# Paired 64-row score products, one reciprocal for two rows and a reordered seam in a decoder-layer kernel

## The chip, the cores and the metric

The kernel runs on one core of a Trainium2 chip. The metric is the device time of one execution in microseconds (us); the median of the runs counts. A difference is given with an interval where several rounds were run.

## What is computed

One decoder layer on 1024 tokens of width 1024, everything in float32. An input projection feeds two mixers. The first is sparse attention: 8 heads in 2 groups of 4, head size 64, with a compressed branch (63 keys), a selected branch and a window branch (512 keys back), each head and branch with its own gate. With 16 blocks of 64 keys and 16 blocks selected, the selected branch sees every causal key. The second is latent attention with 8 heads of 96 score dimensions. Then an output projection, a layer norm, a gated feed-forward part of width 2816, a layer norm, and a gated embedding with a third norm. The part that the change touches, cut down:

```python
s = jnp.einsum('bqghd,bkgd->bqghk', qblk, kwb).astype(f32)
bias = -slopes[:, :, None] * dist[:, None, None, :].astype(f32)
p = _masked_softmax(s + bias, mask)
o_win = jnp.einsum('bqghk,bkgd->bqghd', p.astype(vwb.dtype), vwb)
...
o = g[..., 0:1] * o_cmp + g[..., 1:2] * o_slc + g[..., 2:3] * o_win
...
gu = x @ w_up[i]
ffn = (jax.nn.silu(gu[..., :D_FF]) * gu[..., D_FF:]) @ w_down[i]
```

## The kernel before, in words

Products in float32 are made from two parts of each operand, a high part (rounded to fp32r) and a low part (the rest). ScalarE writes the high part (`hi`, L103), VectorE subtracts to get the low part (`lo`, L109), and `mm3` (L120) multiplies high by high, high by low and low by high (L122, L123, L124).

**Sparse heads.** A query tile holds 128 rows for a head of 64: one half has the high part of q, the other half the low part; which half is which goes by the parity of the head (`evac_q`, L308). The key tiles hold the high part twice (`KS[g][0]`, `KW[g][0]`) and the low part twice (`KS[g][1]`, `KW[g][1]`), on both halves (`evac_k`, L320). So the scores of one head take two products of 128 rows: q by the high keys gives high times high plus low times high; q by the low keys gives high times low plus low times low.

**Units and groups.** A unit is one head, one block of 128 queries (`qb`) and one branch (the compressed and the selected branch share one: 64 compressed columns, the "head", stand ahead of `n = 128*(qb+1)` selected ones; the window has up to 640). Four units, the heads of one group, make a Group; there are 32 sparse groups, ordered `qb` 0 to 7 for the first and 7 to 0 for the second head group, and then 16 latent groups. `scores` (L490) takes a score tile `s` of two PSUM banks (there are two such tiles), writes one to three stretches of up to 512 columns with `qk_mm` (L486), and lets VectorE add bias and mask, scale and take the row's minimum in one operation (`fused`, L482). `ex` (L532) is the exponential on ScalarE with a running sum; `Group.sm` (L571) takes the reciprocal of the sum (L581) for the rows that `BATCH` (L44) names and then has GpSimd multiply each unit's row by it and by the gate (`scale`, L537). 

**The order of the work.** Every engine works its instructions off in the order in which the program writes them. `pipeline` (L799) writes it: for each unit its scores, then `sm` of the unit before, then the hooks (pieces of the latent projections spread over the units, L840 to L882), then a slice of an older group, then `ex`. The slices (L620) of a group come from two units after its last unit on (`LAG`), a quarter of its steps per unit; a step is four transposes (`tr`, L587; the transposes are L594), the split of the result on ScalarE and VectorE, and, two steps later, its two products with the values (`pvm`, L607; L614 and L616).

**The seam.** After attention comes the output projection by blocks of 128 tokens (`out_proj`, L957) and then the feed-forward part as a list `seq` of products `u_prod(i, n)` (L1082), each of 12 matmuls of 512 columns. It works with sums and differences of blocks of x and of the weights. The loop at L1281 writes, for each place `k` in the list: the product, the evacuation of the one before (`u_evac`, L1094), and then what the steps ahead need. At k=2 come the transposes of the last token block and two differences (`tr_x1`, `t_sums`), at k=3 two more differences on VectorE (`t_more`, L1017), at odd k the split of the weight that is used three to seven places later (`u_split`, L1059), then the jobs due at k (`jobs`, L1206): splits of x blocks (`put`, L1022: ScalarE L1029, VectorE L1031), weight fetches (`u_fetch`, L1040, on SP's DMA queue) and weight sums on GpSimd (`u_sum`, L1046). `u_fetch(1)` is due at k=6 and `u_fetch(2)` at k=11; the sums of `u_fetch(1)` are split at k=13 and multiplied from k=15 on.

```python
BATCH = ((0, 1), (1, 2), (2, 3), (3, 4))                              # L44
                u.qk(G, i)                                            # L805
                if prev is not None:
                    prev[0].sm(prev[1])
...
        elif k == 3:                                                  # L1288
            t_more(NB - 1, dve)
        if k % 2 and k // 2 + 2 < SKEW:
            u_split(k // 2 + 2, "g")
        jobs(k)
```

Of the kernel before, what the change touches and what calls it, by code (L numbers as in the profile page):

```python
# [14 lines left out]
T = 1024  # L15
# [52 lines left out]
def body(tc, sb, dr, A, out, dbg, stop):  # L68
# [414 lines left out]
        dve.tensor_tensor_reduce(out=W, in0=ps, in1=bias, op0=OP.add, op1=OP.min, scale=scale, scalar=LOWEST,  # L483
                                 accum_out=m)

    def qk_mm(ps, terms, c0, c1):  # L486
        for i, (q, k) in enumerate(terms):
            pe.matmul(ps, q, k[:, c0:c1], start=i == 0, stop=i == len(terms) - 1)  # L488

    def scores(W, n, terms, head, bias, scale, st, hbias=None, WH=None):  # L490

        S = psum["pool"].tile([128, 2, 512], F32, name="s", tag="s", bufs=2)
        nch = 1 if head + n <= 512 else 2
        w = n // nch
        if head + w > 512:
            pc = bank()
            qk_mm(pc[:, :head], terms, 0, head)
            ph, off = pc[:, :head], 0
        else:
            ph, off = S[:, 0, :head], head  # L500
        for c in range(nch):
            if c == 0 and off:
                qk_mm(S[:, 0, :off + w], terms, 0, head + w)
            else:
                qk_mm(S[:, c, off:off + w], terms, head + c * w, head + c * w + w)
        if head:
            fused(WH, ph, hbias, scale, st[:, 0:1])
        m = st[:, 1:2] if head else st[:, 0:1]
        if nch == 1:
            fused(W[:, :n], S[:, 0, off:off + w], bias, scale, m)  # L510
        else:
            fused(W[:, :n].rearrange("p (c w) -> p c w", c=2), S[:, :, off:off + w],
                  bias.rearrange("p (c w) -> p c w", c=2), scale, m)

    class Unit:

# [5 lines left out]
        def qk(self, G, i):  # L522
            k = self.k
            if G.st is None:
                G.st = small([128, 24], "st", 4)
            self.low, self.sum, self.inv = [G.st[:, (4 * z + i) * k:(4 * z + i + 1) * k] for z in range(3)]
            self.W = slot(n=self.n)
            self.WH = small([128, 64], "wh", 12) if self.head else None
            self.rows = [self.WH, self.W] if self.head else [self.W]
            self._qk(self)  # L530

        def ex(self):  # L532
            for m, w in enumerate(self.rows):
# [8 lines left out]
    def nsa_unit(g, hh, qb, br):  # L542
        h = 4 * g + hh
        slope = 2.0 ** -(h + 1)
        k0 = max(0, qb - 4)
        n = 128 * (qb + 1) if br == 0 else 128 * (qb + 1 - k0)
        gt = gate[:, qb, 3 * h:3 * h + 3]

        def qk(u):
            q = QS[h][:, qb * 128:qb * 128 + 128]  # L550
            if br == 0:
                scores(u.W, n, [(q, KS[g][0]), (q, KS[g][1])], 64, Ds[:, T - n:], slope, u.low,
                       Dc[:, 56 - 8 * qb:120 - 8 * qb], u.WH)
            else:
                scores(u.W, n, [(q, KW[g][0][:, k0 * 128:]), (q, KW[g][1][:, k0 * 128:])], 0,
                       Dw[:, WIN + 128 - n:], slope, u.low)
# [232 lines left out]
    def mla_unit(h, qb):  # L789
        n = 128 * (qb + 1)  # L790

        def qk(u):
            (qh, ql), (kh, kl) = M["q", h], M["k"][h % 2]
            qs = slice(qb * 128, qb * 128 + 128)
            terms = [(qh[:QKD, qs], kh[:QKD, :]), (ql[:QKD, qs], kh[:QKD, :]), (qh[:QKD, qs], kl[:QKD, :])]
            scores(u.W, n, terms, 0, M["tri"][:, T - n:], 1.0, u.low)
        return Unit(n, False, [1.0], False, qk)

    def pipeline(groups, hooks):  # L799
        pend = []  # L800
        t = 0
        prev = None
        for gi, G in enumerate(groups):
            for i, u in enumerate(G.units):
                u.qk(G, i)  # L805
                if prev is not None:
                    prev[0].sm(prev[1])
                for hk in hooks.get((gi, i), []):
                    hk()
                while pend and pend[0][0] <= t:  # L810
                    pend.pop(0)[1]()
                u.ex()
                prev = G, i
                t += 1
            for k, s in enumerate(slices(G, 4)):
                pend.append((t + LAG + k, s))
        prev[0].sm(prev[1])
        while pend:
            pend.pop(0)[1]()
        while held:  # L820
            pvm()

    groups = []
    for g in range(2):
# [20 lines left out]
    def lv(h, kb):  # L845
        return lambda: M["v", h // 4, kb // 2][:, kb % 2, h % 4, :, :].rearrange("p a d -> p (a d)")
    NG = len(groups)
    def at_unit(n, fn):
        hook(n // 4, n % 4, fn)

# [430 lines left out]
    for k, (i, n) in enumerate(seq):  # L1281
# [244 lines left out]
```

## Time and profile before

| what | value |
|---|---|
| median of 3 runs | 1441.51 us (1440.3 to 1442.77) |
| the profiled execution: own time | 1443.31 us |
| the profiled execution: span from first to last instruction | 1441.4 us |
| mean granted TensorE clock | 0.993 of full speed |
| busy: TensorE, VectorE, ScalarE, GpSimd | 97%, 70%, 49%, 41% of the span |
| instructions | 20419 |

The profile is one execution. PE is TensorE, PEld its weight loads, DVE VectorE, ACT ScalarE, POOL GpSimd, SP the engine whose queue issues the DMAs. A TensorE matmul is recorded with a modelled end and the next one starts before it, so busy time of PE overstates; the distance from one start to the next tells what a matmul costs. The time lies in stages: up to 172 us the input projections, 172 to 434 the sparse units, 434 to 577 the latent units, then the output projection, from 676 on the feed-forward part.

### The profile page before, as it was taken

The numbers are of one execution on the slowest core, as the hardware profiler recorded it, in microseconds if no ns is written. First come the engines' busy times: TensorE is split into PE (matmuls) and PEld (weight loads), VectorE is DVE, ScalarE is ACT, GpSimd is POOL, SyncE is SP. The second block draws the span as 40 slices with busy tenths as digits, with TensorE's granted clock in tenths as the row PEclk, the third lists the DMA queues.
The fourth block names the chain that finished last, engine by engine and source line by source line (L and its number), as shares of the span: only waits on it lengthen the run. The fifth ranks groups of instructions, "written<-read, shape, count | busy, mean of one in ns | idle before, by whom it ended". The sixth has DMA issues, their size and how long they took to land.

```text
span 1441.4 us, 20419 instructions
## 1 busy us (share of the span) xinstructions
PE 1398.6 (97%) x7066; PEld 1174.8 (82%) x7066; DVE 1008.9 (70%) x1928; ACT 707.9 (49%) x1449; POOL 592.7 (41%) x567
## 2 busy tenths in 40 slices
PE   8999989999989999999999999999999999999997
PEld 8987868888868888788788888888888888888886
DVE  5367589999989898667856455555555655686765
ACT  3323499888888888233632333332334533342221
POOL 2311155554543337204264577677683021021331
PEclk9999999999999999999999999999999999999999
DMA  7022000000000014224233345565455965761001
GB/s 278 16 85 69 26 1 23 1 1 1 16 16 1 1 34 132 70 88 146 74 124 123 119 170 188 197 222 188 154 215 186 377 241 204 250 217 60 30 33 56
DMA packets 66488, 159.84 MB, mean 111 GB/s; under 512 B 8017, under 2 KB 8657, under 8 KB 66385
## 3 DMA queue, kind: packets, MB, share of 16 engines
q1 hardware_dynamic: 66384, 158.54, 31.7%
q8 instruction: 56, 0.92, 0.3%
q14 instruction: 48, 0.39, 0.1%
HBM read 118.40 MB, written 40.11 MB: 110 GB/s over the span
## 4 chain that ended last, share of the span: by engine, by line
PE 70%; DVE 12%; POOL 7%; issue 5%; ACT 4%; DMA 1%; SPq 0%; DVEq 0%; POOLq 0%; ACTq 0%
PE p L124 18%; PE p L122 18%; PE p L123 18%; PE s L488 6%; PE p L594 5%; DVE b L111 3%; PE p L616 2%; PE p L614 2%; DVE h L111 2%; DVE b L483 1%; ACT b L534 1%; ACT h L105 1%; POOL b L1163 1%; POOL b L1159 1%; POOL h L1139 1%
## 5 line engine op out<-in xcount | busy, mean ns | idle before, releaser
L122 PE MATMUL p<-b 128*128 128x512 f32 (+3 forms) x1524 | 583.2, 383 | 6.2 <-POOL b L107 4.3
L124 PE MATMUL p<-b 128*128 128x512 f32 (+3 forms) x1524 | 582.0, 382 | 5.6 <-DVE b L111 5.5
L123 PE MATMUL p<-b 128*128 128x512 f32 (+3 forms) x1524 | 580.6, 381 | 0.0
L111 DVE TENSOR_TENSOR b<-b 128x1024 fp32r<-128x1024 f32 (+4 forms) x177 | 230.0, 1317 | 162.5 <-ACT b L105 129.6
L124 PEld LDWEIGHTS p<-b 128*128 128x128 f32 x1524 | 287.7, 189 | 63.0 <-DVE b L111 9.8
L122 PEld LDWEIGHTS p<-b 128*128 128x128 f32 x1524 | 287.7, 189 | 60.3 <-POOL b L107 4.3
L123 PEld LDWEIGHTS p<-b 128*128 128x128 f32 x1524 | 287.7, 189 | 51.6 <-DVE b L111 0.3
L111 DVE TENSOR_TENSOR h<-p,h 128x512 fp32r<-128x512 f32 (+1 forms) x244 | 148.5, 627 | 10.4 <-ACT h L105 9.0
L534 ACT ACTIVATE b<-b,st 128x640 f32<-128x640 f32 (+7 forms) x192 | 142.9, 744 | 12.8 <-DVE st L483 10.2
L483 DVE CUSTOM_DVE_ANT_0 b<-s,b 128x640 f32<-128x640 f32 (+7 forms) x192 | 137.6, 717 | 9.5 <-PE s L488 6.3
L105 ACT ACTIVATE h<-p 128x512 fp32r<-128x512 f32 (+1 forms) x244 | 130.7, 550 | 21.8 <-PE p L594 19.3
L105 ACT ACTIVATE b<-b 128x1024 fp32r<-128x1024 f32 (+2 forms) x139 | 120.8, 880 | 31.1 <-POOL b L1057 10.5
L107 POOL TENSOR_SCALAR b<-b 128x1024 fp32r<-128x1024 f32 (+3 forms) x45 | 54.9, 1225 | 197.5 <-DMA b<-in_pT 45.6
L594 PE MATMUL p<-ident,b 128*128 128x128 f32 x816 | 129.5, 275 | 5.8 <-DVE b L740 1.9
L1097 ACT ACTIVATE h<-p 128x512 f32<-128x512 f32 x66 | 39.3, 596 | 194.5 <-PE p L124 194.5
L539 POOL TENSOR_SCALAR b<-b,st,gate 128x640 f32<-128x640 f32 (+7 forms) x128 | 101.4, 793 | 74.3 <-DVE st L581 41.5
L594 PEld LDWEIGHTS p<-ident,b 128*128 128x128 f32 x816 | 99.8, 141 | 26.5 <-POOL b L539 4.4
L488 PE MATMUL s<-b 128*128 128x320 f32 (+10 forms) x480 | 104.0, 336 | 6.6 <-DVE st L483 2.9
L105 ACT ACTIVATE b<-kk 128x1024 fp32r<-128x1024 f32 x62 | 65.1, 1058 | 83.9 <-DMA kk<-td 44.2
L614 PE MATMUL p<-h,b 128*128 128x512 f32 x228 | 103.8, 455 | 1.1 <-DVE h L111 0.9
L488 PEld LDWEIGHTS s<-b 96*128 96x128 f32 (+1 forms) x480 | 81.3, 190 | 20.6 <-DVE st L483 5.8
L909 POOL TENSOR_TENSOR ls<-ls,half 128x1 f32<-128x1 f32 x24 | 18.6, 774 | 183.6 <-DVE ls L908 183.6
(180 smaller groups left out, 1741.4 us busy)
## 6 DMA issues: line engine op xcount, KB each, us to landing
b<-in_wup SPq DMA_DIRECT2D x49, 512.0 KB, 5.0
kk<-hd SPq DMA_DIRECT2D x62, 256.0 KB, 4.5
hd<-h SPq DMA_DIRECT2D x57, 256.0 KB, 2.0
b<-in_wdown SPq DMA_DIRECT2D x22, 512.0 KB, 4.6
td<-b SPq DMA_DIRECT2D x44, 256.0 KB, 2.7
kk<-td SPq DMA_DIRECT2D x40, 256.0 KB, 4.5
kk<-in_wdown SPq DMA_DIRECT2D x22, 256.0 KB, 5.1
hd<-kk SPq DMA_DIRECT2D x20, 256.0 KB, 2.9
```

The lines of the kernel that those rows point to most:

```text
L105: act.activation(h, x, AF.Copy)
L107: pool.tensor_scalar(h, x, 1.0, 1.0, op0=OP.mult, op1=OP.mult)
L111: dve.tensor_sub(l, x, f(h))
L122: pe.matmul(ps, ah, bh, start=start, stop=False, skip_group_check=more)
L123: pe.matmul(ps, ah, bl, start=False, stop=False, skip_group_check=more)
L124: pe.matmul(ps, al, bh, start=False, stop=stop, skip_group_check=more)
L483: dve.tensor_tensor_reduce(out=W, in0=ps, in1=bias, op0=OP.add, op1=OP.min, scale=scale, scalar=LOWEST, accum_out=m)
L488: pe.matmul(ps, q, k[:, c0:c1], start=i == 0, stop=i == len(terms) - 1)
L534: act.activation(w, w, AF.Exp, bias=self.low[:, m:m + 1], scale=-1.0, accum_out=self.sum[:, m:m + 1])
L539: pool.tensor_scalar(w, w, self.inv[:, m:m + 1], self.gates[m], op0=OP.mult, op1=OP.mult)
L594: pe.transpose(pt[:rows, i * 128:i * 128 + 128], u.WH if col < 0 else u.W[:, col:col + rows], ident)
L614: pe.matmul(ch.bank[:, c], v, th, start=start, stop=tl is None and ch.left == 0)
```

## The change

It does four things. The scores of two sparse heads are written together: `scores` now returns three pieces, and at even units `pipeline` writes the first products of both heads, then the second products of both in turn, stretch by stretch, and the fused operation of the first head; the fused operation of the second head stands where it stood. The second product of a head works only on the 64 rows that hold the high part of its q (so low times low falls away): rows 0 to 63 for the even head, 64 to 127 for the odd one. `BATCH` takes the reciprocal for two units at once, in all groups. In the seam, `t_more` moves from k=3, ahead of the split, to k=4, behind it; and the fetches of weights 1 and 2 go through ScalarE's DMA queue. A block that builds the groups is moved ahead of `pipeline` unchanged, and latent units are written as before.

```diff
-BATCH = ((0, 1), (1, 2), (2, 3), (3, 4))
+BATCH = ((0, 2), (2, 4))
...
-    def qk_mm(ps, terms, c0, c1):
-        for i, (q, k) in enumerate(terms):
-            pe.matmul(ps, q, k[:, c0:c1], start=i == 0, stop=i == len(terms) - 1)
...
+        def first():
+            for ps, c0, c1 in parts:
+                for i, (q, k) in enumerate(terms[:-1]):
+                    pe.matmul(ps, q, k[:, c0:c1], start=i == 0, stop=False)
+
+        def last(ps, c0, c1):
+            q, k = terms[-1]
+            return lambda: pe.matmul(ps, q, k[:, c0:c1], start=False, stop=True)
+
+        def rest():
+            if head:
+                fused(WH, ph, hbias, scale, st[:, 0:1])
...
+        return first, [last(*x) for x in parts], rest
...
+            r = slice(64 * (hh % 2), 64 * (hh % 2) + 64)
             if br == 0:
-                scores(u.W, n, [(q, KS[g][0]), (q, KS[g][1])], 64, Ds[:, T - n:], slope, u.low,
-                       Dc[:, 56 - 8 * qb:120 - 8 * qb], u.WH)
...
+                return scores(u.W, n, [(q, KS[g][0]), (q[r], KS[g][1][r])], 64, Ds[:, T - n:], slope, u.low,
+                              Dc[:, 56 - 8 * qb:120 - 8 * qb], u.WH)
...
             for i, u in enumerate(G.units):
-                u.qk(G, i)
+                if gi >= NG:
+                    first, last, rest = u.qk(G, i)
+                    first()
+                    for fn in last:
+                        fn()
+                    rest()
+                elif i % 2 == 0:
+                    two = [G.units[j].qk(G, j) for j in (i, i + 1)]
+                    for first, last, rest in two:
+                        first()
+                    for ab in zip(*[x[1] for x in two]):
+                        for fn in ab:
+                            fn()
+                    two[0][2]()
+                else:
+                    two[1][2]()
...
-                nc.sync.dma_start(RAW[i][j], A["wup"][i, :, j, :])
+                (act if 0 < i < 3 else nc.sync).dma_start(RAW[i][j], A["wup"][i, :, j, :])
...
-        elif k == 3:
-            t_more(NB - 1, dve)
         if k % 2 and k // 2 + 2 < SKEW:
             u_split(k // 2 + 2, "g")
+        if k == 4:
+            t_more(NB - 1, dve)
         jobs(k)
```

## Rows read from the trace of the kernel before

**Rows 1.** The page, part 1: engine, busy us, share of the span, instructions.

```profile
PE 1398.6 (97%) x7066; PEld 1174.8 (82%) x7066; DVE 1008.9 (70%) x1928; ACT 707.9 (49%) x1449; POOL 592.7 (41%) x567
```

**Rows 2.** Busy time by stretch: length; PE, PEld, DVE, ACT, POOL (instructions); clock, DMA.

```profile
172.00:200.00 28.00, 20.88 (x113) 15.79 (x112) 21.17 (x113) 22.86 (x84) 16.24 (x34) 0.94 0.01 1
200.00:300.00 100.00, 97.82 (x606) 83.43 (x604) 96.98 (x277) 91.69 (x222) 57.30 (x76) 1.00 0.03 9
300.00:390.00 90.00, 88.42 (x544) 77.60 (x543) 87.52 (x284) 77.77 (x195) 44.52 (x65) 1.00 0.02 7
390.00:434.00 44.00, 36.63 (x215) 28.83 (x214) 38.10 (x146) 36.16 (x110) 20.14 (x39) 0.96 0.04 13
434.00:577.00 143.00, 140.79 (x873) 118.07 (x872) 128.23 (x347) 122.03 (x273) 62.05 (x70) 1.00 0.14 43
...
900.00:1000.00 100.00, 98.91 (x435) 81.21 (x435) 55.87 (x47) 32.03 (x47) 73.81 (x48) 1.00 0.56 197
```

**Rows 3.** Timeline of PE from 340 us: start, us, engine, line, what.

```profile
340.29 0.75 PE L488 MATMUL s<-b 128*128 128x320 f32 x4
340.88 0.34 PE L122 MATMUL p<-b,h 128*128 128x384 f32 x1
```

**Rows 4.** Timeline of PE from 443 us: narrow and half-width products.

```profile
443.09 0.28 PE L124 MATMUL p<-b 128*128 128x256 f32 x1
443.23 0.41 PE L122 MATMUL p<-b 128*64 128x512 f32 x1
...
447.65 0.27 PE L616 MATMUL p<-h,b 128*128 128x128 f32 x1
447.76 0.91 PE L488 MATMUL s<-b 96*128 96x512 f32 x3
```

**Rows 5.** Groups of DVE, 200 to 390 us, and its timeline from 340 us.

```profile
L581 DVE RECIPROCAL st<-st 128x1 f32<-128x1 f32 (+1 forms) x82 | 13.0, 159 | 0.2 <-ACT b L534 0.2
...
340.84 0.16 DVE L581 RECIPROCAL st<-st 128x1 f32<-128x1 f32 x1
340.92 0.67 DVE L111 TENSOR_TENSOR h<-p,h 128x512 fp32r<-128x512 f32 x1
```

**Rows 6.** The page, part 5: the scaling of the sparse rows on POOL.

```profile
L539 POOL TENSOR_SCALAR b<-b,st,gate 128x640 f32<-128x640 f32 (+7 forms) x128 | 101.4, 793 | 74.3 <-DVE st L581 41.5
```

**Rows 7.** Timeline of 237 to 240 us: a unit's scores and the fused operations.

```profile
237.63 0.76 PE L488 MATMUL s<-b 128*128 128x320 f32 x4
...
238.56 0.67 DVE L111 TENSOR_TENSOR h<-p,h 128x512 fp32r<-128x512 f32 x1
...
239.15 0.81 DVE L483 CUSTOM_DVE_ANT_0 b<-s,b 128x640 f32<-128x640 f32 x1
```

**Rows 8.** Timeline of the seam, 684 to 698 us.

```profile
684.53 1.20 SPq L1044 DMA_DIRECT2D b<-in_wup  x2
...
687.21 1.22 DVE L111 TENSOR_TENSOR b<-b 128x1024 fp32r<-128x1024 f32 x1
...
691.37 1.46 POOL L1053 TENSOR_TENSOR b<-b 128x512 f32<-128x512 f32 x1 [11.09 <-DMA b<-in_wup]
...
691.57 1.05 ACT L105 ACTIVATE b<-b 128x1024 fp32r<-128x1024 f32 x1
...
691.59 1.79 DVE L1019 TENSOR_TENSOR kk<-kk 128x512 f32<-128x512 f32 x1
...
694.99 2.28 DVE L111 TENSOR_TENSOR b<-b 128x1024 fp32r<-128x1024 f32 x1
...
696.16 2.26 POOL L1057 TENSOR_TENSOR b<-b 128x512 f32<-128x512 f32 x1
...
697.33 0.80 PE L124 MATMUL p<-b 128*128 128x512 f32 x1 [3.09 <-DVE b L111]
```

**Rows 9.** Busy time by stretch at the seam, columns as in Rows 2.

```profile
696.00:700.00 4.00, 2.67 (x6) 2.15 (x7) 4.00 (x6) 2.77 (x7) 2.42 (x2) 0.57 0.00 0
700.00:704.00 4.00, 4.00 (x12) 3.09 (x11) 4.00 (x10) 3.52 (x9) 0.00 (x0) 0.57 0.00 0
```

More of the change, by code (lines that the diff above doesn't have):

```diff
@@ L494, in scores @@
         w = n // nch
+        parts = []
         if head + w > 512:
-            pc = bank()
-            qk_mm(pc[:, :head], terms, 0, head)
-            ph, off = pc[:, :head], 0
+            ph, off = bank()[:, :head], 0
+            parts.append((ph, 0, head))
         else:
@@ L502, in scores @@
             if c == 0 and off:
-                qk_mm(S[:, 0, :off + w], terms, 0, head + w)
+                parts.append((S[:, 0, :off + w], 0, head + w))
             else:
[L505 to L513, printed above, removed]
+                parts.append((S[:, c, off:off + w], head + c * w, head + c * w + w))
+        def first():
[8 more added lines that the diff above has]
+                fused(WH, ph, hbias, scale, st[:, 0:1])
+            m = st[:, 1:2] if head else st[:, 0:1]
+            if nch == 1:
+                fused(W[:, :n], S[:, 0, off:off + w], bias, scale, m)
+            else:
+                fused(W[:, :n].rearrange("p (c w) -> p c w", c=2), S[:, :, off:off + w],
+                      bias.rearrange("p (c w) -> p c w", c=2), scale, m)
+        return first, [last(*x) for x in parts], rest
     class Unit:
@@ L550, in qk @@
             q = QS[h][:, qb * 128:qb * 128 + 128]
+            r = slice(64 * (hh % 2), 64 * (hh % 2) + 64)
             if br == 0:
-                scores(u.W, n, [(q, KS[g][0]), (q, KS[g][1])], 64, Ds[:, T - n:], slope, u.low,
-                       Dc[:, 56 - 8 * qb:120 - 8 * qb], u.WH)
-            else:
-                scores(u.W, n, [(q, KW[g][0][:, k0 * 128:]), (q, KW[g][1][:, k0 * 128:])], 0,
-                       Dw[:, WIN + 128 - n:], slope, u.low)
+                return scores(u.W, n, [(q, KS[g][0]), (q[r], KS[g][1][r])], 64, Ds[:, T - n:], slope, u.low,
+                              Dc[:, 56 - 8 * qb:120 - 8 * qb], u.WH)
+            return scores(u.W, n, [(q, KW[g][0][:, k0 * 128:]), (q[r], KW[g][1][r, k0 * 128:])], 0,
+                          Dw[:, WIN + 128 - n:], slope, u.low)
         if br == 0:
@@ L795, in qk @@
             terms = [(qh[:QKD, qs], kh[:QKD, :]), (ql[:QKD, qs], kh[:QKD, :]), (qh[:QKD, qs], kl[:QKD, :])]
-            scores(u.W, n, terms, 0, M["tri"][:, T - n:], 1.0, u.low)
+            return scores(u.W, n, terms, 0, M["tri"][:, T - n:], 1.0, u.low)
         return Unit(n, False, [1.0], False, qk)
[L799 to L804, printed above, removed]
-                u.qk(G, i)
[L806 to L821, printed above, removed]
     groups = []
@@ L847, in body, with pipeline @@
     NG = len(groups)
+    def pipeline(groups, hooks):
+        pend = []
+        t = 0
+        prev = None
+        for gi, G in enumerate(groups):
+            for i, u in enumerate(G.units):
+                if gi >= NG:
[12 more added lines that the diff above has]
+                    two[0][2]()
+                else:
+                    two[1][2]()
+                if prev is not None:
+                    prev[0].sm(prev[1])
+                for hk in hooks.get((gi, i), []):
+                    hk()
+                while pend and pend[0][0] <= t:
+                    pend.pop(0)[1]()
+                u.ex()
+                prev = G, i
+                t += 1
+            for k, s in enumerate(slices(G, 4)):
+                pend.append((t + LAG + k, s))
+        prev[0].sm(prev[1])
+        while pend:
+            pend.pop(0)[1]()
+        while held:
+            pvm()
     def at_unit(n, fn):
```

2 lines of the change are left out of this document (1 added, 1 removed).

## The prediction

> **What bounds the kernel.** I read the page's busy shares first, then busy time by stretch, then timelines. Over the span TensorE is busy 97%, VectorE 70% [rows 1], which looks like a kernel bound by TensorE alone. By stretch it is not so [rows 2]. From 200 to 390 us (sparse units with many keys) VectorE is busy 96.98 of 100 and 87.52 of 90 us: only 3.02 + 2.48 = 5.5 us are left, and TensorE's records fill as much. Whatever the change takes from TensorE there, the stretch can shrink only by those 5.5 us and by what is taken from VectorE. From 172 to 200 and 390 to 434 us (few keys) nobody is full, VectorE 76% and 87%: there the latency of a unit's chain counts. From 434 to 577 us TensorE is busy 140.79 of 143 us and the bound. The seam is a place by itself: TensorE stands 3.09 us until VectorE's split at L111 ends [rows 8], and behind that stall the granted clock is 0.57 over 8 us [rows 9].
>
> **1. The seam.** At k=3 VectorE runs the two differences of `t_more` and then the low part of weight 3. The differences take from 691.59 to 694.99, 3.40 us, the split 2.28 us, and TensorE goes on at 697.33 [rows 8]. Both are slow because GpSimd's additions run beside them (691.37 to 698.4): the same split took 1.22 us at 687.21 [rows 8]. The change puts the split ahead. Its high part on ScalarE ends at 691.57 + 1.05 = 692.62 [rows 8], so the low part runs from 692.62 to 693.84 at 1.22 us, or to 694.90 at 2.28; TensorE's last product ahead of the wait starts about 3.48 us before 697.33 (3.09 us idle and a modelled end of 0.39), so it wants the low part at 693.85 + 0.23 = 694.08. The stall becomes 0, or 0.8 at most. `t_more` at k=4 feeds a `put` at k=5 whose product stands at k=13, eight products of 12 x 0.23 = 2.8 us later: covered.
>
> The moved fetch decides which of the two durations holds. GpSimd starts its additions when the weight has landed (released by the DMA [rows 8]); SP issued it at 684.53, since nothing of k=3 to 6 stood ahead of it. On ScalarE's queue `u_fetch(1)` stands behind all of ScalarE's work up to k=6, so after 697 us, and the additions come after the critical splits. They are due at k=13, seven products or 19 us after k=6. SP's queue loses two pairs of fetches and nothing behind them starts later. ScalarE gets four issues, 1.20 us for two [rows 8], 2.4 us in sum; it is half idle [rows 1]. If a buffer isn't free at k=11, ScalarE stands there and evacuations queue behind it: up to one product, 2.8 us.
>
> The clock: 8 us at a mean of 0.57 [rows 9] is 2 x (1 - 0.57) x 8 = 6.9 us at the 1.2 GHz level, 1.3 of them still in the stall; the other 5.6 us of work would take half at 2.4 GHz, so 2.8 us go back. It fell after TensorE had stood 3.09 us [rows 8]; with no such stall left I count on it staying up. Sum: **-3.1 - 2.8 = -5.9 us**, ends -3 and -6.5.
>
> **2. The reciprocals.** VectorE goes on 0.08 us after a reciprocal starts (340.84 to 340.92 [rows 5]); the recorded 159 ns overlap with the next operation. Of 82 in the full stretch [rows 5] half fall away: 41 x 0.08 = **-3.2 us** there, VectorE being full. The others (23 in the sparse stretches with few keys, 32 in the latent stage) lie beside other work. Price: the scaling of the first unit of a pair waits for the second. GpSimd then has two scalings in a row, 0.79 us each [rows 6], ahead of the transposes. Behind them on GpSimd stand the latent row scalings and weight splits, which nobody awaits soon. The cover is the lag of two units, 2 x 262/128 = 4.1 us, against 1.6 us (more where 64 columns are scaled too). So nothing with many keys. With few keys, 12 groups (qb 0 to 2, both branches, both head groups) may each pay one scaling: 0 to 12 x 0.79 = 9.5 us. I take a third, **+3 us**, as VectorE is 76 to 87% busy there [rows 2] and fills part of it.
>
> **3. The second products.** In the FFN 435 products of 512 columns pass in 100 us [rows 2]: 0.23 us each, 0.45 ns a column; 320 columns take (340.88 - 340.29)/4 = 0.147 us [rows 3]. There are 208 second products, 71,680 columns, 33 us. No row shows two products on different row halves. Bounds: nothing gained (they pass one after the other as now); all at once, 16.5 us of TensorE. Between them lies a floor that rows show: 128 columns take 0.11 us (447.65 to 447.76 [rows 4]), not 0.06, which fits a weight load per product. With two loads, a pair of stretches costs no less than 0.22 us: nothing is gained at up to 192 columns, 0.07 at 320, 0.13 at 384, 0.19 at 448, 0.23 at 512; summed over the stretches of all 64 pairs 11 us. I take 11, by the nearest row. But the stretch is full on VectorE too: of the 5.5 us left there I count **-2 us**.
>
> What could a change between 128 rows and 64 cost? The nearest row is a change from 128 to 64 columns: L122 on 64 columns starts 0.14 us after a product of 256 columns [rows 4], against 0.12 by the rate: 0.02 us. With 128 changes that is 2.6 us of TensorE, inside the 11. The upper bound is a product's whole tail, 0.34 us recorded less 0.17 by the rate [rows 3]: 0.17 us.
>
> **4. The order of the pair** is moved past one unit's slice. The second head's first product needs the score tile that the unit before still holds until its fused operation ends. I price that as a rival, and it is why I take 2 of 5.5 us above.
>
> **5. Latent units** keep their order; 32 reciprocals less, ends -2.5 and 0, taken **-0.5 us** as TensorE is the bound.
>
> **Sum.** -5.9 - 3.2 + 3 - 2 - 0.5 = -8.6 us. The profiled execution took 1443.3 us (1.9 more than its span, 1.8 above the median of 1441.5): 1434.7 by it, 1432.9 against the median. I say 1433.
>
> **Rivals.**
> *Lost look-ahead (slower).* At 237.63 TensorE starts a unit's scores while VectorE's fused operation of the unit before ends only at 238.56; VectorE takes the new scores at 239.15 [rows 7]. In the new order the other head's first products (0.29 us) can start only at 238.56, then come the second products of both (0.44) and some 0.2 us until VectorE sees them: 239.49, 0.34 us late. If all 64 pairs pay that, 22 us; with the gains of 1, 2 and 5 (9.6 us) 1454 us. It decides from (9.6 + 2.9)/64 = 0.20 us a pair on. For it: both engines are full, so a hole is not made up. Behind the waiting product stand, on TensorE, the slice's transposes and value products, and on them wait ScalarE's and VectorE's splits. Against: VectorE has the subtractions of the slice before to fill the hole (0.67 us each in [rows 5]; here it had one from 238.56 on), and where a slice has two steps they cover it; and a VectorE that is late finds its scores ready.
> The Trainium skill (TensorE: Matmul & The Clock Gate, Part 3) says matmuls on different row groups start about 4 ns apart; no row here shows it. By it the 0.44 would be 0.30 and the hole 0.20 us, just at the deciding point.
>
> *A drain at each change (slower).* If TensorE empties at each change of rows, 128 x 0.17 = 21.8 us, less the 11 gained: +10.8 us of TensorE in a full stretch; with the seam and 5, 1441.5 - 6.4 + 10.8 = 1446. The 0.02 us of [rows 4] speak against it.
> The Trainium skill (TensorEngine Tiling (Array Packing), Tiling Modes) states that changing the tiling mode drains TensorE; for a change of columns the trace does not agree, 0.02 us and not 0.17.
>
> *The halves don't run at once.* TensorE saves nothing, term 3 is 0 and scores come later: about 1439.
>
> *The seam only moves.* GpSimd's additions or a blocked ScalarE queue stall TensorE a few places later and the clock falls there: 1433 + 6 = 1439.
>
> *Everything is used.* VectorE's idle time goes and few keys cost nothing: 1433 - 3.5 - 3 - 2 = 1424.5.
>
> **Chances.** Forecast 0.50 (0.46 of it faster), lost look-ahead 0.13, drain 0.06, halves one after the other 0.14 (0.05 faster), seam moved 0.10 (0.05 faster), everything used 0.07. A measurement tells 0.2%, 2.9 us. Faster by more: 0.46 + 0.05 + 0.05 + 0.07 = 0.63; within: 0.18; slower: 0.19. The range runs from 1424.5, everything used, to 1445, leaving out most of the slower cases.
>
> **What would show it.** Seam: no wait of L124 on L111 near 694 us, granted clock 1.00 there, L1019 and the split back at 0.7 and 1.2 us, L1053 after 700 us. Reciprocals: 96, of two units. Pair: second products of two heads starting closer than 0.147 us; 128 to 64 rows without a gap. Look-ahead: VectorE's idle time between 200 and 390 us released by L488. Wrong I am if VectorE's idle time there grows above 12 us, or TensorE stands at the seam for over 1 us.

## The result, and the profile after

The changed kernel takes 1484.7 us (median of 4 runs, 1482.3 to 1486.5) against 1442.1 us for the kernel before beside it: a ratio of 1.0296, 95% interval [1.0283, 1.0309]. It is slower by 3%, where 1433 was forecast and 1445 was the upper end. Its profiled execution took 1482.3 us, span 1480.4 us. Two executions among the experiments, one each of two kernels, had a granted clock of 0.75 from end to end and took 1734 us; no comparison below rests on them.

The page of the changed kernel, part 1, answers to [rows 1]:

```profile
PE 1414.4 (96%) x7066; PEld 1157.9 (78%) x7066; DVE 1009.9 (68%) x1828; ACT 709.4 (48%) x1449; POOL 589.1 (40%) x567
```

VectorE has 100 instructions less (96 reciprocals and 4 guards) and 1 us more of busy time, TensorE 15.8 us more, and the span grew by 39. All the busy shares fell: most of the time went into waits. The same stretches as in [rows 2], changed kernel:

```profile
172.00:200.00 28.00, 21.41 (x77) 13.55 (x77) 15.49 (x86) 18.59 (x70) 12.02 (x27) 0.70 0.01 1
200.00:300.00 100.00, 85.60 (x505) 60.69 (x503) 82.16 (x219) 78.60 (x193) 47.56 (x68) 1.00 0.03 9
300.00:390.00 90.00, 80.47 (x475) 61.74 (x475) 77.91 (x216) 66.98 (x165) 39.49 (x56) 0.98 0.00 1
```

From 200 to 390 us VectorE is busy 82.16 + 77.91 = 160.1 of 190 us; before it was 184.5. Both engines that were full now stand idle in turn. In the first stretch the granted clock also fell, to 0.70 from 0.94 [rows 2]. How much the sparse stage lost in all is read at one instruction, the fused operation of the first latent score. In the timelines of VectorE, first the kernel before:

```profile
427.94 0.28 DVE L483 CUSTOM_DVE_ANT_0 b<-s,b 128x128 f32<-128x128 f32 x1
```

and the changed kernel:

```profile
469.49 0.28 DVE L483 CUSTOM_DVE_ANT_0 b<-s,b 128x128 f32<-128x128 f32 x1
```

The sparse stage ends 41.6 us later; the span is 39.0 us longer. So all of the loss, and a little more, arises before 470 us, and the seam gives some back. The start of this instruction, called "first latent score" below, is the yardstick of the experiments. It carries 1 to 2 us of scatter, since the first score of the stage itself starts between 172.5 and 174.1 us from run to run.

What the engines wait for in the sparse stage is in the waits of the changed kernel, 172 to 470 us (waiting engine, tile and line, releaser: us in total, times, longest):

```profile
ACT h L105 <- PE p L603: 42.7, 65, 3.4
...
PE s L507 <- DVE st L483: 29.7, 43, 1.8
...
DVE b L483 <- PE s L511: 16.0, 26, 1.2
PEld s L507 <- DVE st L483: 15.4, 21, 1.6
```

L507 are the first score products, L511 the second ones, L483 the fused operations, L603 the transposes. It is a ring: TensorE waits for a fused operation to release a score tile, and VectorE's next fused operation waits for the second products behind it. One turn, in the timeline of the changed kernel from 245.7 us:

```profile
245.73 0.69 DVE L111 TENSOR_TENSOR h<-p,h 128x512 fp32r<-128x512 f32 x1
...
245.99 0.45 PE L507 MATMUL s<-b 128*128 128x320 f32 x2
...
246.48 0.95 DVE L483 CUSTOM_DVE_ANT_0 b<-s,b 128x768 f32<-128x768 f32 x1
...
247.59 0.53 PE L507 MATMUL s<-b 128*128 128x320 f32 x2 [1.14 <-DVE st L483]
248.05 0.56 PE L511 MATMUL s<-b 64*128 64x320 f32 x4
...
248.75 0.82 DVE L483 CUSTOM_DVE_ANT_0 b<-s,b 128x640 f32<-128x640 f32 x1 [0.60 <-PE s L511]
```

At 245.99 TensorE writes the even head of a pair into one score tile. The other tile still holds the odd head of the pair before, whose fused operation runs only at 246.48, behind the even head's own operations and a subtraction of the slice (245.73). TensorE stands 1.14 us, with the slice's transposes and value products queued behind. Then the second products of both heads come last, so VectorE stands 0.60 us too.

The seam went the other way. Stretches of the kernel before, from the first product after the transposes of x1, in two parts (84 products, then up to the same later product), columns as in [rows 2]:

```profile
685.04:710.73 25.69, 22.60 (x87) 17.75 (x86) 22.77 (x37) 17.07 (x36) 6.98 (x4) 0.87 0.18 60
710.73:792.33 81.60, 81.60 (x361) 67.57 (x360) 51.17 (x57) 30.15 (x52) 43.17 (x28) 1.00 0.36 120
```

and the same work in the changed kernel:

```profile
728.55:748.05 19.50, 19.50 (x87) 15.75 (x86) 17.76 (x33) 14.82 (x32) 3.01 (x2) 1.00 0.23 79
748.05:831.25 83.20, 82.23 (x361) 67.42 (x360) 56.58 (x62) 32.19 (x55) 45.88 (x31) 1.00 0.36 119
```

The first part is 6.19 us shorter, without idle time of TensorE and at a clock of 1.00. The second is 1.60 us longer. Why, in the timeline of the changed kernel:

```profile
736.15 1.23 DVE L111 TENSOR_TENSOR b<-b 128x1024 fp32r<-128x1024 f32 x1 [0.97 <-ACT b L105]
...
738.56 0.69 DVE L1044 TENSOR_TENSOR kk<-kk 128x512 f32<-128x512 f32 x1
...
739.29 0.39 ACTq L1069 DMA_DIRECT2D b<-in_wup  x1
...
744.96 1.40 POOL L1078 TENSOR_TENSOR b<-b 128x512 f32<-128x512 f32 x1 [21.18 <-DVE b L1056]
...
749.08 3.62 DVE L1056 TENSOR_TENSOR b<-b 128x256 fp32r<-128x256 f32 x4
...
754.48 0.50 PE L124 MATMUL p<-b 128*128 128x512 f32 x1 [0.37 <-DVE b L111]
...
759.37 3.02 DVE L1056 TENSOR_TENSOR b<-b 128x256 fp32r<-128x256 f32 x4
...
763.58 0.50 PE L124 MATMUL p<-b 128*128 128x512 f32 x1 [0.60 <-DVE b L111]
```

The split of the weight takes 1.23 us and not 2.28, the difference behind it 0.69 and not 1.79 [rows 8]: GpSimd's additions begin only at 744.96. Being late, they run beside later splits: four of x blocks (L1056) take 3.62 and 3.02 us there, where four take 1.42 us at 757.43 without additions beside them. The split of a weight behind each comes late by that, and TensorE stands 0.37 and 0.60 us.

### The profile page after: what moved, and what is told of

Read it like the earlier page. It is cut to its first block, busy times and chain, and to the rows that moved or that the text cites. A ratio compares the mean times of both kernels' runs of the same rounds, so it can differ in the third digit from the quotient of the medians.

```text
span 1480.4 us, 20319 instructions
## 1 busy us (share of the span) xinstructions
PE 1414.4 (96%) x7066; PEld 1157.9 (78%) x7066; DVE 1009.9 (68%) x1828; ACT 709.4 (48%) x1449; POOL 589.1 (40%) x567
## 4 chain that ended last, share of the span: by engine, by line
PE 65%; DVE 13%; POOL 8%; issue 8%; ACT 4%; DMA 1%; SPq 0%; DVEq 0%; ACTq 0%; POOLq 0%
PE p L122 16%; PE p L124 16%; PE p L123 16%; PE p L603 5%; PE s L507 4%; PE s L511 3%; DVE b L111 3%; DVE b L483 2%; PE p L623 2%; DVE h L111 2%; PE p L625 2%; ACT h L105 2%; POOL b L1188 1%; POOL b L1184 1%; POOL h L1164 1%
## 5 line engine op out<-in xcount | busy, mean ns | idle before, releaser
L483 DVE CUSTOM_DVE_ANT_0 b<-s,b 128x640 f32<-128x640 f32 (+7 forms) x192 | 137.7, 718 | 26.2 <-PE s L511 22.0
L603 PE MATMUL p<-ident,b 128*128 128x128 f32 x816 | 134.0, 282 | 3.0 <-POOL b L548 1.5
L603 PEld LDWEIGHTS p<-ident,b 128*128 128x128 f32 x816 | 98.8, 143 | 35.4 <-issue 8.2
L507 PE MATMUL s<-b 128*128 128x320 f32 (+10 forms) x288 | 74.5, 350 | 22.3 <-DVE st L483 19.8
L111 DVE TENSOR_TENSOR b<-kk,b 128x1024 fp32r<-128x1024 f32 x62 | 76.7, 1256 | 19.8 <-ACT b L105 19.2
```

The costliest lines, as they stand in the source:

```text
L111: dve.tensor_sub(l, x, f(h))
L507: pe.matmul(ps, q, k[:, c0:c1], start=i == 0, stop=False)
L603: pe.transpose(pt[:rows, i * 128:i * 128 + 128], u.WH if col < 0 else u.W[:, col:col + rows], ident)
```

## The experiments

Each kernel is the changed one or the one before with one part undone or done alone. The kernels made from the changed code have its line numbers.

**The changed kernel in the old order, on 128 rows** (what is left: merged reciprocals, seam).

```diff
-                if gi >= NG: ... elif i % 2 == 0: ...
+                first, last, rest = u.qk(G, i)
+                first()
+                for fn in last: fn()
+                rest()
-  (q[r], KS[g][1][r])      (q[r], KW[g][1][r, k0 * 128:])
+  (q, KS[g][1])            (q, KW[g][1][:, k0 * 128:])
```

> The changed kernel with the scores of the sparse heads written as before: one unit at a time, second product on 128 rows. The reciprocal for two rows, the later t_more and the fetches on ScalarE's queue stay. Lost look-ahead (the pair has to wait for both score tiles): the sparse stage falls back to its old length less some 3 us, with the seam 1432 to 1438 us. Rival, the batched reciprocal (scalings come later and the transposes wait): the sparse stage stays 20 us or more above, 1455 to 1480. Rival, a drain at each change of rows: 1432 to 1438 too, so this run separates only the batch.

Measured: 1446.9 us, ratio 1.0032 [1.0018, 1.0046]; first latent score at 435.30, 7.4 us late. That lies between the two theories: the merged reciprocals cost, and most of the 41.6 us is elsewhere.

**The same with the second products on 64 rows**, each head finished before the next: only the first minus and plus lines of the diff above. The product of the two low parts is left out, as in every kernel here on 64 rows.

> As the run before, but the second product works on the 64 rows (low times low left out), one head at a time in the old order. Lost look-ahead: only the changes between 128 and 64 rows are left, about 0.09 us each in the trace of the changed kernel, 256 of them, 23 us of TensorE of which part lies beside VectorE: 1440 to 1455. Drain as the main cause: as slow as the changed kernel or slower, 1475 to 1490.

Measured (one run): 1471.6 us, first latent score at 458.67, 23.4 us behind the run before and above what the first theory expected. Here TensorE goes to 64 rows and back for each of 128 heads, 256 changes. In the timeline of TensorE, two second products of one head and the first transpose behind them:

```profile
243.59 0.64 PE L511 MATMUL s<-kk,b 64*128 64x448 f32 x2
244.17 0.33 PE L603 MATMUL p<-ident,b 128*128 128x128 f32 x1
```

The products of 448 and 384 columns take 0.58 us, where 0.37 would do at 0.45 ns a column: about 0.10 us is added behind each product on 64 rows, whether the next one has 64 rows or 128. With 0.09 us for each way into 64 rows (step 3 below), that is 128 x 0.09 + 208 x 0.10 = 32 us of TensorE's time, of which a part is covered. The clock cost time too: it was 0.50 from 182 to 202 us, against 0.70 and 1.00 in the two halves of that stretch in the run before. That is 14 us more at the 1.2 GHz level, an estimate of up to 7 us of loss. How the 23.4 us divide among these is not shown.

**The changed kernel on 128 rows**: pair order, merged reciprocals, no row halves.

```diff
-  (q[r], KS[g][1][r])      (q[r], KW[g][1][r, k0 * 128:])
+  (q, KS[g][1])            (q, KW[g][1][:, k0 * 128:])
```

> The changed kernel with the pair order kept and the second products on all 128 rows again. Lost look-ahead: the wait stays and the two heads' second products pass one after the other, 0.15 us or more later each pair: 1485 to 1500. Drain: the loss goes, 1435 to 1450.

Measured (one run): 1479.4 us, first latent score at 466.81, a little less than the first theory expected and far more than the second. Against the old order (435.30), both with merged reciprocals, that is 31.5 us for the order alone, 31.5/64 = 0.49 us a pair; against the changed kernel (469.49) the row halves cost another 2.7, little more than the scatter. Its waits from 172 to 470 us show the ring without any 64-row product:

```profile
PE s L507 <- DVE st L483: 31.0, 46, 1.9
...
DVE b L483 <- PE s L511: 15.5, 25, 1.4
PEld s L507 <- DVE st L483: 15.4, 20, 1.6
```

**The odd head's fused operation moved to the even unit**, the rest as changed.

```diff
                     two[0][2]()
-                else:
-                    two[1][2]()
+                    two[1][2]()
```

> The changed kernel with one line moved: the fused operation of the second head follows that of the first at the even unit, ahead of the slice's subtractions on VectorE, so both score tiles are free two slices before the next pair wants them. Lost look-ahead: TensorE's idle time ahead of the first products (30 us on L483) goes almost wholly, the sparse stage is at or below its old length: 1428 to 1446. Drain or batch: 1470 to 1485.

Measured: 1467.4 us, 1.0179 [1.0164, 1.0195]; first latent score at 455.27, 14.2 us earlier than in the changed kernel. Issuing one operation earlier gives back a third of the loss. That is less than the theory expected, by which the sparse stage would have been as short as before.

**The seam edits alone** on the kernel before.

```diff
-                nc.sync.dma_start(RAW[i][j], A["wup"][i, :, j, :])
+                (act if 0 < i < 3 else nc.sync).dma_start(RAW[i][j], A["wup"][i, :, j, :])
-        elif k == 3:
-            t_more(NB - 1, dve)
+        if k == 4:            # behind the split
+            t_more(NB - 1, dve)
```

> The kernel before with the two edits of the seam alone (t_more at k=4, fetches 1 and 2 on ScalarE's queue). If the seam's gain stands by itself and the loss of the run with the old score order came from the reciprocal for two rows: 1442 - 4.5 = about 1437 to 1439, sparse and latent stages as before within 1 us. If the seam's gain is wholly given back later: 1441 to 1443.

Measured: 1439.5 us, 0.9981 [0.9972, 0.9990]; first latent score at 427.94, as before. From the first product after the transposes, the first 84 products take 19.44 us in place of 25.69, the next part 83.27 in place of 81.60: -6.2 and +1.7.

**The seam edits and a merged reciprocal for the first pair of each group only.**

```diff
-BATCH = ((0, 1), (1, 2), (2, 3), (3, 4))
+BATCH = ((0, 2), (2, 3), (3, 4))
```

> As the run before, with one reciprocal for the first two units of a group and single ones for the third and fourth. If the batch costs time because the last pair's two scalings stand in a row ahead of the transposes (POOL on the chain): this batch delays no transpose, the sparse stage is 0 to 2 us shorter than with single reciprocals, 1435 to 1438. If any later scaling costs time: half of the 9.8 us of the full batch stays, 1441 to 1444.

Measured: 1444.6 us, 1.0018 [1.0009, 1.0027]; first latent score 4.6 us behind the seam edits alone. Most of the 7.4 us of both pairs is already in the first pair, though its scalings have two units more of cover than the last pair's. The trace has the sparse transposes waiting for scalings, 7.9 us on TensorE's weight loads from 172 to 470 us against 3.5 with the seam edits alone; why with that much cover is not settled.

**Each seam edit by itself**: only the transfers on ScalarE's queue, then only `t_more` moved.

> The kernel before with fetches 1 and 2 on ScalarE's queue alone. If GpSimd's additions beside VectorE made the split late: VectorE takes 0.7 us for each difference and 1.2 us for the split, the stall at L124 falls from 3.1 us to below 1.5 us, the clock stays up, the FFN starts some 4 to 5 us earlier relative to the transposes before it: 1436 to 1440. If the order on VectorE made it: the stall stays above 2 us and 1441 to 1443.

> The kernel before with t_more at k=4 behind the split alone. If the order on VectorE made the split late: the stall falls below 1 us, 1436 to 1440. If GpSimd's additions made it: the split still takes 2.3 us, a stall of 0.5 to 1.5 us at this place and another one a few products later, where the differences of 1.8 us now stand ahead of the next split, 1438 to 1442.

Measured (one run each): 1438.3 and 1436.6 us. The transfers alone shorten the first 84 products by 6.1 us and give 1.55 back later; the moved differences alone shorten them by 4.0 and give nothing back. The two are not added up: either takes the collision away, and the net is -4 to -4.6 us with any of them.

**Pair order with both fused operations at the even unit, 128 rows, single reciprocals, seam**, and **the same on 64 rows**.

```diff
-BATCH = ((0, 2), (2, 4))
+BATCH = ((0, 1), (1, 2), (2, 3), (3, 4))
-                else:
-                    two[1][2]()
+                    two[1][2]()
-  (q[r], KS[g][1][r])      (q[r], KW[g][1][r, k0 * 128:])     (128-row kernel only)
+  (q, KS[g][1])            (q, KW[g][1][:, k0 * 128:])
```

> The same kernel as the pair order with both fused operations at the even unit on 128 rows (its one profile had a granted clock of 0.75 from end to end, against 0.99, and can't be set beside the others). Theory (the lost look-ahead is the cost of the pair order): the first latent score 5 to 15 us later than before, end at 1440 to 1452. Rival (two score tiles are too few for a pair in any order): 20 us or more. Beside its twin on 64 rows, which came 17.9 us late there and took 1456.4 us: if the row halves pay, this one is slower than that; if the 128 changes at 0.09 us cost about what the halves give, it is within 4 us.

> As the run before (both fused operations at the even unit, one reciprocal a unit), with the second products on 64 rows, two heads on the two halves; they leave out the product of the low parts. Theory (128 changes of rows cost 0.09 us each, 11.6 us, and the halves that run at once give about as much back): within 4 us of the run before. Rival (the changes cost nothing once look-ahead is back, since the product that waits is covered): 5 us or more below it. Rival (the halves hardly help): 8 us or more above it.

Measured: 128 rows 1454.7 us, 1.0089 [1.0066, 1.0113], first latent score at 444.67; 64 rows 1456.4 us (one run), 445.81. Neither theory holds as put: 16.7 us of the pair order stay, between "5 to 15" and "20 or more". Waits of the 128-row kernel, 172 to 470 us:

```profile
ACT h L105 <- PE p L603: 28.7, 46, 2.8
...
PEld p L625 <- DVE h L111: 12.5, 18, 1.2
...
PE s L507 <- DVE st L483: 8.4, 15, 1.9
...
PEld s L507 <- DVE st L483: 5.9, 12, 0.8
```

The waits of the first products fell from 31.0 + 15.4 to 8.4 + 5.9 us. What remains are evacuations waiting for transposes and value products (L625) waiting for evacuations. A reading is that eight products in a row leave ScalarE and VectorE without transposes, and then TensorE without splits; that is argued, not tested. The halves change the stage by 1.1 us: nothing that can be told from scatter.

**Scalings issued late**, on the seam edits: the even unit's scaling stands behind the odd unit's reciprocal.

```diff
-                    for u in us:
-                        u.scale()
+                    if i % 2:
+                        for u in self.units[i - 1:i + 1]:
+                            u.scale()
```

> The kernel before with both seam edits, and one reciprocal a unit at its own time, as before; only the scalings of an even unit wait until those of the odd one are issued. Nothing is saved, so all that differs is how late the scaled rows come. Theory (the merged reciprocal costs by the lateness of the scalings on GpSimd, which the transposes and the latent row scalings wait for): the first latent score comes 5 to 8 us later than with the seam edits alone, and the time is 1444 to 1448. Rival (what costs is the guard and the reciprocal itself, queued on VectorE one unit later ahead of a fused operation): the same as the seam edits alone, within 1.5 us.

Measured: 1437.5 us, 0.9975 [0.9966, 0.9985], no cost. But it does not test lateness, as its theory thought: around 240 us each scaling starts 0.12 us later than in the seam kernel, and so does everything else. GpSimd waits only for the reciprocal that it reads; moving a scaling in the program, with nothing of GpSimd's between, moves nothing. It takes away the order of issue as a cause.

**The even unit's reciprocal late too**, two single reciprocals at the odd unit's place.

```diff
-                    dve.reciprocal(r, s)
-                    for u in us:
-                        u.scale()
+                    if i % 2:
+                        for x in (i - 1, i):
+                            dve.reciprocal(self.st[...x...], self.st[...x...])
+                            self.units[x].scale()
```

> The seam edits alone, with one reciprocal a unit as before, but the even unit's reciprocal and its scalings stand where the odd unit's do. No instruction is merged or saved; only the even unit's scaled rows are late, by what the merged form makes them. Theory (the merged reciprocal costs by lateness, not by its form): the first latent score 6 to 9 us later than with the seam edits alone, 1445 to 1450. Rival (it costs by the form: one operation that waits for two heads' sums): within 2 us of the seam edits alone, 1437 to 1441.

Measured: 1447.1 us, 1.0042 [1.0027, 1.0057]; first latent score at 433.46, 5.5 us behind the seam edits alone. Nothing is merged here, and the time is that of the merged kernel (1446.9): the cost is lateness of the scalings, which also come in one piece, and not the merged form. In the old-order kernel with merged reciprocals, timelines of VectorE and GpSimd:

```profile
236.67 0.17 DVE L590 RECIPROCAL st<-st 128x4 f32<-128x4 f32 x1
...
236.94 0.40 POOL L548 TENSOR_SCALAR wh<-wh,st,gate 128x64 f32<-128x64 f32 x1 [2.32 <-DVE st L590]
237.31 0.98 POOL L548 TENSOR_SCALAR b<-b,st,gate 128x768 f32<-128x768 f32 x1
238.27 0.39 POOL L548 TENSOR_SCALAR wh<-wh,st,gate 128x64 f32<-128x64 f32 x1
238.64 0.98 POOL L548 TENSOR_SCALAR b<-b,st,gate 128x768 f32<-128x768 f32 x1
```

GpSimd idles 2.32 us for the reciprocal, then has 2.7 us of scalings in one piece. Who waits, 172 to 430 us of that kernel:

```profile
PEld p L603 <- POOL b L548: 11.0, 16, 1.1
...
PE p L603 <- POOL b L548: 6.4, 13, 0.9
...
PEld p L698 <- POOL b L688: 4.0, 4, 1.8
...
PE p L698 <- POOL b L688: 2.7, 3, 1.6
```

L603 are the sparse transposes, L688 the latent row scalings, which stand behind the scalings in GpSimd's queue, and L698 the latent transposes that read them. The kernel with late single reciprocals, 172 to 470 us (its line numbers are one higher):

```profile
PEld p L604 <- POOL b L548: 10.0, 14, 1.1
...
PE p L604 <- POOL b L548: 5.7, 11, 0.9
```

**A lag of three units** in place of two, with the merged reciprocals (old order, 128 rows, seam) and with the seam edits alone.

```diff
-LAG = 2
+LAG = 3
```

> The merged reciprocals with both seam edits (old unit order, 128 rows), and the transposes of a group one unit later than before (a lag of 3 units in the place of 2). Theory (the transposes wait for late scalings): the 17 us of waits of the transposes on GpSimd's scalings fall to under 6 us and most of the 5 to 7 us comes back, 1437 to 1442, and the saved reciprocals may then show as up to 3 us. Rival (the loss is on GpSimd or VectorE themselves, or in the latent row scalings, whose due times stay): 1444 or more.

> The seam edits alone with the lag of 3 units: what the lag does by itself. The transposes there wait 5 us on GpSimd's scalings in the sparse stage, so at most that is to be had; a longer way to the end of the stage costs about one unit, 3 us, once or twice: 1436 to 1443.

Measured: 1443.9 us, 1.0014 [1.0005, 1.0023], and 1443.8 us, 1.0009 [1.0000, 1.0019]; first latent scores at 427.07 and 425.86. With the transposes one unit later most of the sparse loss of the merged form is gone (435.30 to 427.07, 1.2 us behind its twin with single reciprocals, which is scatter or a rest), and so are nearly all waits of the sparse transposes. So the waits fell as the theory expected, but the time is the rival's, 1444. Merged kernel with the longer lag, 172 to 470 us:

```profile
PEld p L698 <- POOL b L688: 4.2, 5, 1.7
...
PE p L698 <- POOL b L688: 2.6, 3, 1.4
...
PEld p L603 <- POOL b L548: 0.7, 3, 0.3
```

The latent transposes wait as long as before (L698), so it is the sparse ones whose waits cost the time up to the first latent score. The longer lag loses about 4 us of its own between the last latent score and the first transpose of x1 (36.7 and 37.4 us, with and without merged reciprocals, against 33.2 and 32.9 with a lag of two). And the two kernels take the same time: 96 reciprocals fewer show no gain where the sparse lateness is covered. Whether they are worth nothing, or their worth goes into the waits of the latent transposes (4.2 us against 0.2 on the weight loads of its twin), is not shown.

**The moved differences alone, in more runs.**

```diff
-        elif k == 3:
-            t_more(NB - 1, dve)
+        if k == 4:            # behind the split
+            t_more(NB - 1, dve)
```

> The kernel before with only the seam split moved up, all transfers on SyncE's queue as before. In the one look at it the stretch behind the transposes was 4 us shorter, nothing was given back later, and the start fell 2.8 us early by itself. Theory (the edit is worth the 4.0 us of that stretch): 1436.5 to 1439.5, a ratio of about 0.997, a little below the version with both seam edits. Rival (the late transfers of the two raw tiles make it give back the 1.6 us of the other version): a ratio of 0.998 or above.

Measured: 1438.9 us, 0.9980 [0.9971, 0.9989]. The stretch is 4.0 us shorter and nothing comes back (the next part takes 81.60 us, as before), so the trace is the theory's, though the ratio ends where the rival's begins: a ratio to three digits can't tell the two apart. Its seam in the timeline of TensorE:

```profile
699.45 0.50 PE L124 MATMUL p<-b 128*128 128x512 f32 x1 [1.92 <-DVE b L111]
```

and in busy time by stretch, columns as in [rows 2]:

```profile
682.88:704.58 21.70, 19.79 (x88) 15.66 (x86) 20.13 (x34) 15.84 (x34) 6.44 (x4) 1.00 0.21 71
```

TensorE still stands 1.92 us, but the clock of the stretch is 1.00.

All the kernels that keep the old order, the lag of two, 128 rows and reciprocals at their own time, and take one or both seam edits, beat both kernels of this study by about 0.2% or a little more; the three intervals that were taken overlap.

The loss at the first latent score, taken from kernel to kernel: 7.4 (merged reciprocals, in the old order) + 31.5 (order, beside merged reciprocals) + 2.7 (row halves) = 41.6 us. As differences along one path the terms give the whole by themselves; on another path they differ. With both fused operations at the even unit and 64 rows, merged reciprocals in place of single ones cost 9.5 us (455.27 against 445.81). In the merged one of these two the sparse transposes wait for scalings, 172 to 470 us:

```profile
PEld p L603 <- POOL b L548: 10.1, 21, 1.1
```

In the changed kernel itself they hardly do:

```profile
PEld p L603 <- POOL b L548: 1.7, 6, 0.6
```

How much of its loss the merged reciprocals make is not shown, only what they cost in two other orders. Part of the loss also comes by way of the clock: 0.70 against 0.94 over 28 us is 13 us more at the 1.2 GHz level, by an estimate up to 7 us of the loss; no run separates it.

From there to the transposes of x1 the changed kernel loses another 2.0 us (the old-order kernel with merged reciprocals 2.5 us, the seam edits alone 1.2), and the seam gives -6.2 + 1.6: 41.6 + 2.0 - 4.6 = 39.0, the growth of the span.

## Why the prediction was wrong, by its steps

**What bounds the kernel** was read rightly. That a hole is not made up where TensorE and VectorE are both full stands in the prediction too, but only under a rival, and not in the sum.

**Step 4, the order of the pair, is the step that failed.** It stood as the rival "Lost look-ahead" with a chance of 0.13, and in the sum only as the 3.5 us by which the gain of step 3 was cut. The mechanism was named as it came (the second head's first product waits for the tile that the unit before still holds), and its sign that the forecast is wrong, VectorE's idle time of over 12 us from 200 to 390 us, came with 29.9 us. Two things were misjudged. The argument against it, that VectorE has the slice's subtractions to fill the hole, has the direction wrong: those subtractions stand ahead of the odd head's fused operation and make the tile free later, which is a part of the 1.14 us of the timeline. And the price of 0.34 us a pair took one release in the kernel before; the order costs 0.49 us a pair, of which moving the odd fused operation forward takes 14.2 us in 64 pairs, 0.22 each. The rest, 16.7 us with single reciprocals, was in no step, and its cause stays open; that the work of two units comes in one piece on each engine is argued above, not tested. The rival's 1454 us was too low even so: it took 22 us for the order and kept all the gains.

**Step 2, the reciprocals**: priced -3.2 + 3, measured +7.4 us in the sparse stage. "Nothing with many keys" was wrong. The cover was taken as the lag of two units, 4.1 us, against the scalings' 1.6, but the even unit's scalings also wait for the odd unit's exponentials (2.32 us of idle GpSimd in the row of the late-reciprocal experiment), and where 64 columns are scaled too the piece is 2.7 us. "Latent row scalings, which nobody awaits soon" was wrong too, since the transposes of L698 wait 4.0 us for them on the weight loads and 2.7 us on the products (0.4 and none in the kernel before); at the first latent score this costs little, as with the longer lag the same waits stay and the loss does not. The gain of 3.2 us was not found: with the sparse lateness covered by a longer lag the net was 0. Where it goes is not shown.

**Step 5**, -0.5: the stretch from the first latent score to the transposes of x1 grew by 2.0 us. Kernels whose latent units are as before differ by 1.3 us there (+1.2 with both seam edits, -0.1 with the moved differences alone), so no gain is seen, and a loss is not certain.

**Step 3, the second products.** That the halves run at once was right. In the timeline of the changed kernel:

```profile
243.50 0.34 PE L507 MATMUL s<-kk,b 128*128 128x384 f32 x1
...
243.77 0.47 PE L511 MATMUL s<-kk,b 64*128 64x448 f32 x2
...
244.08 0.34 PE L511 MATMUL s<-kk,b 64*128 64x384 f32 x2
...
244.35 0.33 PE L603 MATMUL p<-ident,b 128*128 128x128 f32 x1
```

Two products of 448 columns, each 0.47 us long by the record, end together after 0.47 us: they start 3 to 4 ns apart. The Trainium skill (TensorE: Matmul & The Clock Gate, Part 3) states about 4 ns for matmuls on different row groups, and the trace agrees. But the next two start 0.31 us later and not 0.20. Over 36 such pairs of 320 to 512 columns, start to start to the next pair, a pair takes one product's time and about 0.10 us: 0.253 at 320 columns against 0.147 for one product on 128 rows, 0.33 at 512 against 0.233. The estimate of 0.22 us, a floor of two weight loads, was too low for all of them. A single head's product on 64 rows has the same 0.10 us behind it: the four products here take 0.58 us (243.77 to 244.35), and so do the two of one head in the old order on 64 rows (243.59 to 244.17). So the second head's products come for nothing, and the price is that of 64 rows. And the change from 128 rows to 64 costs 0.27 - 0.17 (384 columns) = 0.1 us in these rows, 0.09 in the middle of 64 of them, not the 0.02 of a change of columns [rows 4]. So the halves save 35,840 columns x 0.45 ns = 16 us, less 104 pairs x 0.105 = 11 (the way back to 128 rows is in these), less 64 x 0.09 = 6: nothing, where 11 us of TensorE were counted. The runs show +1.1 and +2.7 us, both about the scatter.

**The rival "A drain at each change"** took 0.17 us for its price; 0.09 was measured. The Trainium skill (TensorEngine Tiling (Array Packing), Tiling Modes) states that a change of tiling mode drains TensorE; for a change of rows the trace agrees in part, with 0.09 us where a whole tail would be 0.17. It decided nothing here, because it and the concurrent halves cancel.

**Step 1, the seam**, was right in mechanism and size at its place: -5.9 forecast, -6.2 found (3.1 of stall, the rest clock, which stays at 1.00). Of the rival "The seam only moves" a part is true, 1.6 us come back at the two later stalls, so that -4.6 is left.

## What to carry to other kernels

Before the order of producers is changed, list for each buffer who frees it and what is queued ahead of the freeing operation on its engine; here, with two score tiles and both engines over 95% busy, the tiles that came free later cost 0.49 us at each of 64 turns, and one freeing operation issued earlier gave 0.22 of it back. Merging small operations of two units makes the first unit wait for the second: compare that lateness with the cover of everything behind it in the queues, and not only with the saved issue time. Two products on two row halves do run at once, but a pair costs a product and 0.1 us, and the way into 64 rows 0.09: in this kernel, with 64 to 512 columns, it came to nothing.

## What the runs showed of the hardware

- The products of a pair on 64 rows each start 3 to 4 ns apart. Behind a product on 64 rows, alone or in a pair, the next one comes about 0.1 us later than behind one on 128 rows, whether it has 64 rows or 128 (0.25 us and 0.24 against 0.147 at 320 columns). The way from 128 rows to 64 costs 0.09 us.
- After a stall of 3.09 us the granted clock was 0.57 [rows 9]; around one of 1.92 us it stayed at 1.00.
- VectorE's split of 1024 columns took 2.28 us beside GpSimd's additions and 1.23 without, its difference 1.79 and 0.69.
- An operation of GpSimd that is issued later in the program, with nothing of its own queue in between, starts when it did before (scalings issued late: 0.12 us later, as all else around them).
